# Prologue of a one-core transformer-style block: whole-tile fetches, shared squares and a new order for the first two tiles of x

## The chip, the cores and the metric

The kernel runs on one core of one Trainium2 chip. The metric is the time of one execution on the device in microseconds (us); of several runs the median counts. A profiled execution gives one trace, and all times inside the kernel are counted from the first instruction of that trace.

## What is computed

One layer of a hybrid encoder for 512 frames of width 1024, in float32. Only the very beginning matters here: the first norm and the first block of columns of the combined input projection.

```python
def rms_norm(x, gain):
    xf = x.astype(jnp.float32)
    y = xf * lax.rsqrt(jnp.mean(xf * xf, axis=-1, keepdims=True) + RMS_EPS)
    return (y * gain.astype(jnp.float32)).astype(x.dtype)

h = rms_norm(x, mix_norm_pre[layer])
proj = jnp.einsum("bsd,de->bse", h, w_in[layer])
xa, ga, q, k, v, f_logit, g_a, g_b = jnp.split(proj, offs, axis=-1)
xc = causal_dwconv(xa, conv_a_w[layer], conv_a_b[layer])
...
```

## The kernel before

Five engines work side by side: PE multiplies matrices, ACT (ScalarE), DVE (VectorE) and POOL (GpSimd) do the elementwise work, SP issues most DMAs. Each runs its own list of instructions in order. Float32 products are made from three products of a shorter format: an operand is split into a high part (a rounded copy, made by ACT) and a low part (operand minus high part, made by DVE or POOL), and a product is high x high + high x low + low x high.

The 512 frames lie in four tiles of 128 frames (`xts[0]` to `xts[3]`, 128 x 1024 each). For every tile the prologue makes the sum of squares (`sumsq`, `sumsq_whole`: ACT squares with a running sum, then a square root on ACT and a reciprocal on DVE, `rstd_of`, L233 and L235), scales the tile by that and by the gain (`scaled`, L441, DVE, one half of 512 columns at a time), turns the half by four PE transposes into a PSUM bank (`turn`, L242), copies the high part from there (`evac_hi`, L246, ACT, into `hh`) and makes the low part (`evac_lo`, L250, DVE, into `hl`). The names `us[0]` to `us[3]` are the first four blocks of 128 columns of `w_in`; `us[t].hi()` casts (L172, ACT) and `us[t].lo(pool)` subtracts (L175, POOL). `half(i, lo, hi)` is the product of block i with frames lo to hi: 24 matmuls of 256 columns, the ones with the weight's high part at L457 and L458, those with its low part at L460. The first call, `half(0, 0, 256)`, needs tiles 0 and 1 alone.

The gain is a vector along the 1024 columns, and DVE needs it on every partition. `gone` holds the gain in its columns 0 to 1023 and ones in its last 128 columns, on one row; PE multiplies the ones with the gain (L420), so that two PSUM banks (`pgain`) hold it on all 128 partitions. The gain is fetched by a DMA on ACT's queue (L397), which is followed there by the load of the square root's table and a trial square root (`warm`, L398). `spin` (L415) runs matmuls on an identity matrix whose results nobody reads.

In this prologue the order is written out by hand (`manual_schedule`): each engine gets its instructions in the order of the calls, across all engines' lists. The order before, for tiles 0 and 1 (t, g are tile and half): sumsq(0), scaled(0,0), sumsq(1), us[0].hi and lo, scaled(1,0), turn(0,0), spin(3), turn(1,0), scaled(0,1), turn(0,1), high and low part of (0,0), scaled(1,1), turn(1,1), high and low part of (1,0), (0,1) and (1,1), half(0, 0, 256). Tiles 2 and 3 and the other blocks follow. Tiles 0 and 1 are fetched as two halves each, so SP issues four transfers of 256 KB (L402) and after them the first two weights of 512 KB, tiles 2 and 3, two more weights and the table of constants. PSUM has eight banks; four are asked for first, as sums of the four blocks (`pss`), then two for `pgain`, then one for each turned half.

Of the kernel before, what the change touches and what calls it, by code (L numbers as in the profile page):

```python
# [8 lines left out]
F32 = mybir.dt.float32  # L9
F32R = mybir.dt.float32r  # L10
BF16 = mybir.dt.bfloat16
AF = mybir.ActivationFunctionType
ALU = mybir.AluOpType
# [3 lines left out]
P = 128  # L17
S = 512
D = 1024
KD = D // P  # L20
# [43 lines left out]
def kernel(  # L64
# [15 lines left out]
    nc = tc.nc  # L80
    act, dve, pool, pe = nc.scalar, nc.vector, nc.gpsimd, nc.tensor
# [17 lines left out]
    def bank(name):  # L99
        return pspools[-1].tile([P, 512], F32, tag="ps", name=name)  # L100

    xv = x.rearrange("(t p) d -> p t d", p=P)
    ov = out.rearrange("(t p) d -> p t d", p=P)

    HALVES = (slice(0, 512), slice(512, 1024))
# [180 lines left out]
    hh = hpool.tile([P, KD, S], F32R, name="hh")  # L286
    hl = hpool.tile([P, KD, S], F32R, name="hl")
# [30 lines left out]
    with ExitStack() as rg:  # L318
        rt, ixt, tt = {}, {}, {}
        last_act = [None]  # L320
        with ExitStack() as r0:
# [67 lines left out]
            NF = 4  # L389
            with tc.tile_pool(name="pre", bufs=2, side="right", reuse_waits="tile") as pre:  # L390
# [1 line left out]
                man = ExitStack()  # L392
                man.enter_context(tc.manual_schedule())
                warm = small.tile([P, 1], F32, name="warm", bufs=1)
                gone = pre.tile([1, D + P], F32, name="gone", bufs=1)
                pool.memset(gone[:, D:], 1.0)
                act.dma_start(gone[:, :D], gains[0:1, :])  # L397
                act.activation(out=warm, in_=epst, func=AF.Sqrt)  # L398
                xts = [pre.tile([P, D], F32, tag="xt", name=f"xt{t}", bufs=NT) for t in range(NT)]
                for t in range(2):  # L400
                    for c in HALVES:
                        nc.sync.dma_start(xts[t][:, c], xv[:, t, c])  # L402
                us = [Split(*order[t][1:], order[t][0]) for t in range(2)]
                for t in range(2, NT):
                    nc.sync.dma_start(xts[t], xv[:, t])
                us += [Split(*order[t][1:], order[t][0]) for t in range(2, NF)]
                nc.sync.dma_start(cpt, cp)
                emitted[0] = NF
                pss = [bank(f"xa{t}") for t in range(NF)]

                pw = pss[3]

                def spin(n):
                    for i in range(n):
                        pe.matmul(pw[:, P * (i % 4) : P * (i % 4) + P], ident, ident, start=True, stop=True)  # L415
# [8 lines left out]
                def sumsq(t):  # L424
                    xns[t] = pre.tile([P, D], F32, tag="xn", name=f"xn{t}")
                    s2 = small.tile([P, 2], F32, tag="s2", name=f"s2_p{t}")
                    for i, c in enumerate(HALVES):
                        act.activation(out=xns[t][:, c], in_=xts[t][:, c], func=AF.Square, accum_out=s2[:, i : i + 1])
                    ss = small.tile([P, 1], F32, tag="ss", name=f"ss_p{t}")
                    dve.tensor_tensor(out=ss, in0=s2[:, 0:1], in1=s2[:, 1:2], op=ALU.add)  # L430
                    rss[t] = rstd_of(ss, f"p{t}")

                def sumsq_whole(t):
                    xns[t] = pre.tile([P, D], F32, tag="xn", name=f"xn{t}")
                    ss = small.tile([P, 1], F32, tag="ss", name=f"ss_p{t}")
                    act.activation(out=xns[t], in_=xts[t], func=AF.Square, accum_out=ss)
                    rss[t] = rstd_of(ss, f"p{t}")

                def scaled(t, g):
                    c = HALVES[g]  # L440
                    dve.scalar_tensor_tensor(out=xns[t][:, c], in0=xts[t][:, c], scalar=rss[t], in1=pgain[g],  # L441
                                             op0=ALU.mult, op1=ALU.mult)

                def turn(t, g):
                    ptr[t, g] = turn_block(xns[t], t, g, "p")

                def evac_hi(t, g):
                    lasts[0] = turned_hi(ptr[t, g], t, g, hh)

                def evac_lo(t, g):  # L450
                    lasts[1] = turned_lo(ptr[t, g], t, g, hh, hl)

                def half(i, lo, hi):
                    wh, wl = us[i].parts()
                    ps = pss[i][:, lo:hi]
                    for k in range(KD):
                        pe.matmul(ps, wh[:, k], hh[:, k, lo:hi], start=k == 0, stop=False)  # L457
                        pe.matmul(ps, wh[:, k], hl[:, k, lo:hi], start=False, stop=False)  # L458
                    for k in range(KD):
                        pe.matmul(ps, wl[:, k], hh[:, k, lo:hi], start=False, stop=k == KD - 1)  # L460

                sumsq(0)
                scaled(0, 0)
                sumsq(1)
                us[0].hi()
                us[0].lo(pool)
                scaled(1, 0)
                turn(0, 0)
                spin(3)
                turn(1, 0)  # L470
                scaled(0, 1)
                turn(0, 1)
                evac_hi(0, 0)
                evac_lo(0, 0)
                scaled(1, 1)
                turn(1, 1)
                evac_hi(1, 0)
                evac_lo(1, 0)
                evac_hi(0, 1)
                evac_lo(0, 1)  # L480
                evac_hi(1, 1)
                evac_lo(1, 1)
                half(0, 0, 256)
                us[1].hi()
                us[1].lo(pool)
                sumsq_whole(2)
                scaled(2, 0)
                scaled(2, 1)
# [41 lines left out]
            for t in range(NF, TR + NF):  # L530
# [3 lines left out]
                if t < TR:  # L534
                    ps = bank(f"xa{t}")
# [966 lines left out]
```

## Time and profile before

| | us |
|---|---|
| median of three runs | 928.02 (927.01 to 928.88) |
| profiled execution | 926.11 |
| its span, first to last instruction | 924.2 |
| PE busy | 911.7 (99% of the span) |
| DVE, ACT, POOL busy | 685.2, 568.8, 230.6 |

The page of the profile gives busy times, shares and chains of one execution. An engine's row names the source line, the operation, the tile written and the tiles read, and in brackets the idle time before it with what ended that. PEld is the loading of PE's stationary operand, which runs beside its matmuls; names that end in q (SPq, ACTq) are queues that issue DMAs. Several instructions of one line that follow each other are merged in a timeline; the number behind the x counts them.

### The profile page before, as it was taken

To read this page: it belongs to the slowest core of one execution; us is meant where nothing else is said; L and a number is where in the kernel's file an instruction comes from. 1 tells how busy PE (TensorE), PEld (TensorE's weight loads), DVE (VectorE), ACT (ScalarE), POOL (GpSimd) and SP (SyncE) were. 2 spreads that over 40 slices of the span, in tenths; PEclk is the share of its full clock that TensorE was granted. 3 is DMA by queue.
4 is the path that set the end of the run, shared out by engine and by line. 5 is a ranking of instruction groups with operands and counts; after the bars stand their busy time and mean duration, and the time that the engine had idled before them with its cause. 6 is when DMAs were issued, how large, how long until landed. Compare 5 with 4: busy or idle time off the path is not lost.

```text
span 924.2 us, 14992 instructions
## 1 busy us (share of the span) xinstructions
PE 911.7 (99%) x5582; PEld 796.1 (86%) x5582; DVE 685.2 (74%) x1121; ACT 568.8 (62%) x982; POOL 230.6 (25%) x240
## 2 busy tenths in 40 slices
PE   8999999999999999999999999999999999999996
PEld 7988888887888888888888889999999999978885
DVE  5866369632857777777644588999999999889897
ACT  7555495433345566666423376688888888676664
POOL 4134345444242232220111000042323323100001
PEclk9999999999999999999999999999999999999998
DMA  7677589989776566553232755188898888799764
GB/s 278 216 227 208 165 207 256 270 211 253 176 229 152 160 148 157 151 150 86 69 114 91 271 182 163 34 212 235 218 238 204 234 208 211 223 372 325 240 201 142
DMA packets 76282, 182.29 MB, mean 197 GB/s; under 512 B 7281, under 2 KB 35745, under 8 KB 75826
## 3 DMA queue, kind: packets, MB, share of 16 engines
q1 hardware_dynamic: 45056, 123.13, 39.5%
q0 software_dynamic: 30864, 57.68, 30.2%
q8 instruction: 44, 0.72, 0.3%
q10 hardware_dynamic: 290, 0.53, 0.1%
q14 instruction: 28, 0.23, 0.1%
HBM read 148.59 MB, written 33.64 MB: 197 GB/s over the span
## 4 chain that ended last, share of the span: by engine, by line
PE 94%; DVE 2%; DMA 1%; issue 1%; ACT 0%; POOL 0%; SPq 0%; DVEq 0%; POOLq 0%
PE up L924 7%; PE up L922 7%; PE up L921 7%; PE dn L1225 4%; PE dn L1224 4%; PE dn L1223 4%; PE pa L223 2%; PE ga L224 2%; PE ga L223 2%; PE pa L224 2%; PE pa L222 2%; PE ga L222 2%; PE q L222 2%; PE ma L222 2%; PE wo L838 2%; PE mb L222 2%
## 5 line engine op out<-in xcount | busy, mean ns | idle before, releaser
L868 POOL DMA_DIRECT2D ml<-raw_up x41 | 35.0, 855 | 154.8 <-ACT ml L867 79.2
L1076 DVE SCALAR_TENSOR_TENSOR u<-up,cpt,u 128x511 f32<-128x511 f32 x96 | 71.2, 745 | 2.6 <-ACT u L1070 0.9
L1225 PE MATMUL dn<-wh_dn,al 128*128 128x512 f32 x168 | 65.6, 391 | 0.9 <-DVE al L845 0.8
L1224 PE MATMUL dn<-wl_dn,ah 128*128 128x512 f32 x168 | 65.4, 389 | 0.0
L1223 PE MATMUL dn<-wh_dn,ah 128*128 128x512 f32 x168 | 65.4, 389 | 0.0
L921 PE MATMUL up<-sh,th 128*128 128x256 f32 x252 | 60.4, 277 | 0.5 <-ACT x L928 0.5
L922 PE MATMUL up<-sl,th 128*128 128x256 f32 x252 | 60.2, 276 | 0.0
L175 DVE TENSOR_TENSOR wl_dn<-raw_dn,wh_dn 128x1024 fp32r<-128x1024 f32 x42 | 51.5, 1226 | 9.1 <-ACT wh_dn L172 9.1
L172 ACT CAST wh_dn<-raw_dn 128x1024 fp32r<-128x1024 f32 x42 | 44.1, 1050 | 17.5 <-issue 10.3
L845 DVE TENSOR_TENSOR tl<-t,th 128x1024 fp32r<-128x1024 f32 x42 | 51.1, 1218 | 1.3 <-ACT th L902 1.3
L1084 POOL TENSOR_TENSOR yf<-u,u 128x512 f32<-128x512 f32 x24 | 32.0, 1333 | 71.8 <-issue 47.5
L1070 ACT ACTIVATE u<-up,cpt 128x512 f32<-128x512 f32 x48 | 36.9, 778 | 19.8 <-PE up L924 11.0
L921 PEld LDWEIGHTS up<-sh,th 128*128 128x128 f32 x252 | 47.3, 188 | 0.7 <-ACT x L928 0.7
L922 PEld LDWEIGHTS up<-sl,th 128*128 128x128 f32 x252 | 47.3, 188 | 0.0
L902 ACT CAST th<-t 128x1024 fp32r<-128x1024 f32 x42 | 43.9, 1045 | 4.5 <-DVE t L845 1.8
L689 POOL DMA_DIRECT2D B<-maskf x32 | 39.1, 1628 | 27.2 <-DMA B<-cnd 24.1
L922 PE MATMUL up<-h2l,mh 128*128 128x256 f32 x168 | 40.2, 276 | 0.0
L921 PE MATMUL up<-h2h,mh 128*128 128x256 f32 x168 | 40.2, 276 | 0.0
L924 PE MATMUL up<-sh,tl 128*128 128x256 f32 x252 | 38.8, 276 | 0.0
L1225 PEld LDWEIGHTS dn<-wh_dn,al 128*128 128x128 f32 x168 | 31.5, 188 | 8.1 <-DVE al L845 1.7
L175 DVE TENSOR_TENSOR wl_pa<-raw_pa,wh_pa 128x640 fp32r<-128x640 f32 x16 | 13.1, 819 | 32.8 <-ACT wh_pa L172 32.8
L1224 PEld LDWEIGHTS dn<-wl_dn,ah 128*128 128x128 f32 x168 | 31.5, 188 | 6.6
(654 smaller groups left out, 3167.7 us busy)
## 6 DMA issues: line engine op xcount, KB each, us to landing
raw_up<-in_w_up_dram SPq DMA_DIRECT2D x48, 512.0 KB, 5.4
td<-in_w_down_dram POOLq DMA_DIRECT2D x36, 512.0 KB, 5.9
raw_dn<-td SPq DMA_DIRECT2D x24, 512.0 KB, 5.0
B<-cnd POOLq DMA_DIRECT2D x16, 640.0 KB, 4.8
ml<-raw_up POOLq DMA_DIRECT2D x20, 512.0 KB, 5.3
raw_dn<-in_w_down_dram SPq DMA_DIRECT2D x18, 512.0 KB, 3.5
raw_wo<-in_w_out_dram SPq DMA_DIRECT2D x16, 512.0 KB, 3.8
td<-td POOLq DMA_DIRECT2D x12, 512.0 KB, 10.8
```

Source lines behind the costliest of these rows:

```text
L172: act.copy(self.wh, self.raw)
L175: engine.tensor_tensor(out=self.wl, in0=self.raw, in1=self.wh.bitcast(F32), op=ALU.subtract)
L222: pe.matmul(dst, ah, bh, start=first, stop=False)
L845: dve.tensor_tensor(out=out, in0=a, in1=b, op=ALU.subtract)
L902: act.copy(self.th[i], self.t[i])
L921: pe.matmul(dst, wh[:, k], ah[:, k], start=first and k == 0, stop=False, skip_group_check=True)
L922: pe.matmul(dst, wh[:, k], al[:, k], start=False, stop=False, skip_group_check=True)
L924: pe.matmul(dst, wl[:, k], ah[:, k], start=False, stop=k == KH - 1, skip_group_check=True)
L1076: dve.scalar_tensor_tensor(out=c[:, s:], in0=ps[:, : S - s], scalar=col(C_CFW + 3 * e + j), in1=c[:, s:], op0=ALU.mult, op1=ALU.add)
L1223: pe.matmul(dst[t], ah[:, k, tok], wh[:, k], start=first, stop=False, skip_group_check=True)
L1224: pe.matmul(dst[t], ah[:, k, tok], wl[:, k], start=False, stop=False, skip_group_check=True)
L1225: pe.matmul(dst[t], al[:, k, tok], wh[:, k], start=False, stop=last, skip_group_check=True)
```

## The change

Tiles 0 and 1 are fetched by one transfer of 512 KB each. `gone` gets 128 rows: DVE clears columns 0 to 1023 of all of them, the gain is fetched into row 0 behind that, and the ones fill 128 rows, so the vector's matmuls contract over 128 rows of which 127 are zero. Tile 0's squares are made half by ACT and half by DVE (a multiply with a running sum); tile 1's squares are made by ACT in one instruction. Both halves of tile 0 are scaled before anything of tile 1, then turned and copied in that order; `us[0].hi()` and `lo` come next, then tile 1's halves; the four low parts of tiles 0 and 1 come last. The three fillers (six instructions) between transposes go; the four at the start stay. Of the four sums' PSUM banks two are asked for at the beginning and two behind the first product. `half` issues all matmuls with `hh`, then all with `hl`, where it alternated before; their number is the same.

```diff
--- before.py
+++ after.py
@@ -392,23 +392,23 @@
                 man = ExitStack()
                 man.enter_context(tc.manual_schedule())
                 warm = small.tile([P, 1], F32, name="warm", bufs=1)
-                gone = pre.tile([1, D + P], F32, name="gone", bufs=1)
+                gone = pre.tile([P, D + P], F32, name="gone", bufs=1)
+                dve.memset(gone[:, :D], 0.0)
                 pool.memset(gone[:, D:], 1.0)
-                act.dma_start(gone[:, :D], gains[0:1, :])
+                act.dma_start(gone[0:1, :D], gains[0:1, :])
                 act.activation(out=warm, in_=epst, func=AF.Sqrt)
                 xts = [pre.tile([P, D], F32, tag="xt", name=f"xt{t}", bufs=NT) for t in range(NT)]
                 for t in range(2):
-                    for c in HALVES:
-                        nc.sync.dma_start(xts[t][:, c], xv[:, t, c])
+                    nc.sync.dma_start(xts[t], xv[:, t])
                 us = [Split(*order[t][1:], order[t][0]) for t in range(2)]
                 for t in range(2, NT):
                     nc.sync.dma_start(xts[t], xv[:, t])
                 us += [Split(*order[t][1:], order[t][0]) for t in range(2, NF)]
                 nc.sync.dma_start(cpt, cp)
                 emitted[0] = NF
-                pss = [bank(f"xa{t}") for t in range(NF)]
-
-                pw = pss[3]
+                pss = [bank(f"xa{t}") for t in range(2)]
+
+                pw = pss[1]
 
                 def spin(n):
                     for i in range(n):
@@ -424,8 +424,10 @@
                 def sumsq(t):
                     xns[t] = pre.tile([P, D], F32, tag="xn", name=f"xn{t}")
                     s2 = small.tile([P, 2], F32, tag="s2", name=f"s2_p{t}")
-                    for i, c in enumerate(HALVES):
-                        act.activation(out=xns[t][:, c], in_=xts[t][:, c], func=AF.Square, accum_out=s2[:, i : i + 1])
+                    a, b = HALVES
+                    act.activation(out=xns[t][:, a], in_=xts[t][:, a], func=AF.Square, accum_out=s2[:, 0:1])
+                    dve.tensor_tensor_reduce(out=xns[t][:, b], in0=xts[t][:, b], in1=xts[t][:, b], scale=1.0, scalar=0.0,
+                                             op0=ALU.mult, op1=ALU.add, accum_out=s2[:, 1:2])
                     ss = small.tile([P, 1], F32, tag="ss", name=f"ss_p{t}")
                     dve.tensor_tensor(out=ss, in0=s2[:, 0:1], in1=s2[:, 1:2], op=ALU.add)
                     rss[t] = rstd_of(ss, f"p{t}")
@@ -453,36 +455,32 @@
                 def half(i, lo, hi):
                     wh, wl = us[i].parts()
                     ps = pss[i][:, lo:hi]
-                    for k in range(KD):
-                        pe.matmul(ps, wh[:, k], hh[:, k, lo:hi], start=k == 0, stop=False)
-                        pe.matmul(ps, wh[:, k], hl[:, k, lo:hi], start=False, stop=False)
+                    for h in (hh, hl):
+                        for k in range(KD):
+                            pe.matmul(ps, wh[:, k], h[:, k, lo:hi], start=h is hh and k == 0, stop=False)
                     for k in range(KD):
                         pe.matmul(ps, wl[:, k], hh[:, k, lo:hi], start=False, stop=k == KD - 1)
 
                 sumsq(0)
                 scaled(0, 0)
-                sumsq(1)
+                scaled(0, 1)
+                sumsq_whole(1)
+                for g in range(2):
+                    turn(0, g)
+                    evac_hi(0, g)
                 us[0].hi()
                 us[0].lo(pool)
-                scaled(1, 0)
-                turn(0, 0)
-                spin(3)
-                turn(1, 0)
-                scaled(0, 1)
-                turn(0, 1)
-                evac_hi(0, 0)
-                evac_lo(0, 0)
-                scaled(1, 1)
-                turn(1, 1)
-                evac_hi(1, 0)
-                evac_lo(1, 0)
-                evac_hi(0, 1)
-                evac_lo(0, 1)
-                evac_hi(1, 1)
-                evac_lo(1, 1)
+                for g in range(2):
+                    scaled(1, g)
+                    turn(1, g)
+                    evac_hi(1, g)
+                for g in range(2):
+                    for t in range(2):
+                        evac_lo(t, g)
                 half(0, 0, 256)
                 us[1].hi()
                 us[1].lo(pool)
+                pss += [bank(f"xa{t}") for t in range(2, NF)]
                 sumsq_whole(2)
                 scaled(2, 0)
                 scaled(2, 1)
```

## Rows read from the trace of the kernel before

**Rows 1.** Busy time of each engine by stretch; then granted clock and DMA share.
```profile
14.00:918.80 904.80, 900.27 (x5539) 788.24 (x5539) 677.55 (x1106) 559.74 (x964) 227.36 (x231) 1.00 0.70 196
```

**Rows 2.** PE's waits over the whole run: total, times, longest.
```profile
PE up L924 <- DMA ml<-raw_up: 0.9, 1, 0.9
PE dn L1225 <- DVE al L845: 0.8, 1, 0.8
```

**Rows 3.** Chain that ended last, 0 to 16 us: start, duration, what.
```profile
2.13 5.59 DMA xt<-in_x_dram
...
14.00 0.38 PE xa L458
```

**Rows 4.** Timeline of all engines, 0 to 24 us; "x" counts merged instructions.
```profile
0.74 0.53 ACTq L397 DMA_DIRECT2D gone<-in_gains_dram  x1
...
0.74 1.81 SPq L402 DMA_DIRECT2D xt<-in_x_dram  x4
...
1.30 1.28 ACT L398 ACT_TABLE_LOAD   x1 [1.30 <-PEq L1489]
...
3.50 3.78 PE L420 MATMUL gain<-gone 1*128 1x512 f32 x4
...
3.92 0.63 ACT L428 ACTIVATE xn<-xt 128x512 f32<-128x512 f32 x1 [1.12 <-DMA xt<-in_x_dram]
...
4.60 0.63 ACT L428 ACTIVATE xn<-xt 128x512 f32<-128x512 f32 x1
...
6.14 0.75 DVE L441 SCALAR_TENSOR_TENSOR xn<-xt,rs_p,gain 128x512 f32<-128x512 f32 x1
...
7.21 1.11 PE L242 MATMUL tr_p<-ident,xn 128*128 128x128 f32 x4
...
8.11 1.49 PE L415 MATMUL xa<-ident 128*128 128x128 f32 x6
...
8.98 1.04 ACT L172 CAST wh_xa<-raw_xa 128x1024 fp32r<-128x1024 f32 x1
...
10.10 2.37 POOL L175 TENSOR_TENSOR wl_xa<-raw_xa,wh_xa 128x1024 fp32r<-128x1024 f32 x1 [8.67 <-ACT wh_xa L172]
...
11.09 1.08 ACT L246 CAST hh<-tr_p 128x512 fp32r<-128x512 f32 x2 [0.59 <-PE tr_p L242]
...
11.80 1.28 DVE L250 TENSOR_TENSOR hl<-tr_p,hh 128x512 fp32r<-128x512 f32 x2
...
14.06 1.06 ACT L436 ACTIVATE xn<-xt 128x1024 f32<-128x1024 f32 x1
...
14.94 1.12 PE L460 MATMUL xa<-hh,wl_xa 128*128 128x256 f32 x8
...
15.77 1.40 DVE L441 SCALAR_TENSOR_TENSOR xn<-xt,rs_p,gain 128x512 f32<-128x512 f32 x2
...
15.90 0.28 PE L457 MATMUL xa<-hh,wh_xa 128*128 128x256 f32 x1
...
18.78 1.91 PE L242 MATMUL tr_p<-ident,xn 128*128 128x128 f32 x16
```

**Rows 5.** DMA queues to 2.0 us; issues at 1.7 and at 2.5 us, with landing.
```profile
q10 hardware_dynamic: 2, 0.00, 0.8%
...
xt<-in_x_dram SPq DMA_DIRECT2D x1, 256.0 KB, 3.6
...
raw_xa<-in_w_in_dram SPq DMA_DIRECT2D x1, 512.0 KB, 6.4
xt<-in_x_dram SPq DMA_DIRECT2D x1, 256.0 KB, 5.6
```

**Rows 6.** Transposes (L242) of 10.88 to 11.6 us: duration min/median/max, starts.
```profile
L242 PE MATMUL tr_p<-ident,xn x6: 273/273/421, 10.5 to 11.2; 128*128 128x128 f32 x6
```

**Rows 7.** Groups on DVE: line, form, count; busy us, mean ns.
```profile
L175 DVE TENSOR_TENSOR wl_xa<-raw_xa,wh_xa 128x1024 fp32r<-128x1024 f32 x1 | 1.2, 1224 | 2.1 <-ACT wh_xa L172 2.1
...
L719 DVE CUSTOM_DVE_ANT_0 P<-s2c,B 128x512 f32<-128x512 f32 x1 | 0.7, 692 | 0.0
```


## The prediction

> **What bounds the kernel now.** The page's busy table names TensorE (PE) as the bound; I went on to the table of stretches to see where its pauses lie. Between 14.0 and 918.8 us PE works 900.27 of 904.80 us [rows 1]. So whatever the first stage gives PE earlier is kept, unless one of the few later waits takes it. The list of PE's waits has the two largest of those: 0.9 us for a DMA at L924 and 0.8 us for DVE at L1225 [rows 2]; both hang on work that PE's own progress paces, so I expect them to move along with PE.
>
> The change is all in the first 16 us, so there I read the chain of work that ended last [rows 3]. It stands 5.59 us on the transfer of x, then goes through ACT (squares), DVE (scaling of tile 1's first half, of tile 0's second, a low part, scaling of tile 1's second half), PE (transposes), ACT (high part) and DVE (low part) to PE's L458 at 14.00. From there it is PE alone. The timeline gives the two marks that I count with: the first product `half(0, 0, 256)` ends with its eight L460 matmuls from 14.94, and `half(1, 0, 256)` starts at 15.90 [rows 4]. Everything in front of 15.90 is the latency of the first two tiles of x, and the change is worth as much as it moves that mark.
>
> The landing times say which tile is late. Tile 0's first half is issued at 0.74 and has landed when its square starts at 3.92 [rows 4]. The third transfer, tile 1's first half, is issued some 0.9 us after the first and takes 3.6 us [rows 5], to about 5.3; the fourth is issued at 2.13 [rows 3] and takes 5.6 us [rows 5], to 7.7.
>
> The granted clock is 1.00 for 14 to 918.8 us [rows 1]; for the start I read it from matmuls of one form. Four transposes take 1.11 us at 7.21 and sixteen 1.91 us at 18.78, 0.28 against 0.12 us each [rows 4], about a factor of two, as between 1.2 and 2.4 GHz. Around 10.9 us their duration falls from 421 to 273 ns [rows 6], so the clock rises there. Before that rise PE ran fillers, the vector's matmuls at 3.50, transposes, six filler instructions at 8.11 and transposes again.
>
> **The change part by part, against the span of the profiled execution.**
>
> *The vector.* DVE now clears 128 x 1024 before the gains are fetched. No such memset is in the trace. DVE's 128x1024 subtraction at 1.22 us [rows 7] is the nearest row and bounds it above, since it reads two tensors and this reads none; zero bounds it below. I take 1.0, from 0.74 to 1.74; DVE has nothing else to do before tile 0's squares are summed. The 0.53 us trigger on ACT's queue waits for it. Behind it on ACT stand the table load (1.28), `warm` and the first square; the load now starts at 1.30, right behind the trigger [rows 4], and is moved by 1.0 with it; `warm` (under 0.3) ends at 3.8 or 3.9, just before the square's start at 3.92, so this costs nothing. With the memset at 1.22 it would cost 0.2. The transfer itself was done within 1.3 us of its issue (its two packets are counted in the stretch up to 2.0 us [rows 5]), so it lands at 3.0 if nothing stands before it, and at 1.74 + 3.2 = 4.9 if it is served like a half of x (3.92 - 0.74). PE is at the fillers until 3.50 anyway. I take a start of the vector's matmuls at 3.8, nearer to its own row than to x's, with 3.5 and 4.9 as ends. They take 3.78 us in all [rows 4] with 128 rows as with one, since they stream the same 512 columns: first bank ready about 5.9, both at 7.6.
>
> The Trainium skill ("DMA: Bandwidth & Descriptors", section on queues, rings and completion order) says that a DMA engine takes turns between queues, but drains a whole packet of one before it turns to the next. No row shows two queues in competition here. By it the vector would wait behind x, which is the rival "late vector" below.
>
> *Transfers of x.* Two triggers less on SP, some 0.45 us each (four lie between 0.74 and 2.6), so every transfer behind tile 0 is issued 0.45 (x tile 1) to 0.9 us earlier (the weights, tiles 2 and 3). The bytes stay. Tile 0 whole lands between 3.9 (its half) and 4.6 (where the second square could start without waiting); I take 4.4. Tile 1 lands between 5.3 and 7.7; I take 6.5, the middle. The first weight landed at 2.6 + 6.4 = 9.0 [rows 5] and comes at 8.5 to 9.0.
>
> *Tile 0's squares.* ACT's second half (0.63) goes to DVE, whose reduce of 128x512 takes 0.69 (L719, [rows 7]); both run side by side. From the second square's start to the first scaling there are 6.14 - 4.60 = 1.54 us now; so scaling starts at 4.4 + 1.55 = 5.95, when the vector's first bank is just there. The second scaling needs the vector's second bank: 7.6 to 8.35.
>
> *Tile 1.* One square of 128x1024; from such a square's start to its scaling the trace has 15.77 - 14.06 = 1.71 us [rows 4]. 6.5 + 1.7 = 8.2, and DVE is free at 8.35: scalings 8.4 to 9.8. A landing at 7.7 would make it 9.4, which the next step hides but for 0.1 to 0.3 us.
>
> *ACT's order.* After tile 0's second half is scaled, PE turns it at the low clock (1.11, to 9.5), ACT makes the high part (0.59, to 10.1), and then `us[0].hi()` stands in the way: 1.04 us, to 11.1, after which alone tile 1's high parts run (two in 1.08 [rows 4], to 12.1). This is a cost of the new order: the cast used to lie at 8.98, in front of the first high part. Its weight is landed by then, so no DMA wait comes with it; POOL's low part of that weight (behind the cast, 2.4 us [rows 4]) ends at 13.5, just in time for L460.
>
> *DVE's low parts.* Tile 0's first is made at 9.8; the other three follow tile 1's high part at 11.6, 0.6 us apart (two in 1.28 [rows 4]), the last done at 13.45.
>
> *The product.* `half` now issues eight matmuls with hh, eight with hl, eight with the weight's low part, 24 as before. The hh ones run from 11.6 as the high parts arrive, the first four hl ones too; the last four wait for 13.5, take 0.47, then eight L460: 13.5 + 0.47 + 0.96 = 14.9. `half(1, 0, 256)` then starts at 14.9 instead of 15.90: **-1.0 us**. The wait inside the first product, at L458 before 14.00 [rows 3], gives way to the one for 13.5.
>
> *No price.* The later request for two PSUM banks: two sums, two vector halves and four transposed blocks are eight, and the next is wanted at about 17.8, long after the low parts. Fillers gone: PE would be waiting for DVE there anyhow, so they hide nothing but the clock (rival below).
>
> **Sum.** 926.11 (profiled execution, span 924.2 and 1.9 around it) - 1.0 = 925.1. The median lies 1.91 above the profiled execution, so 928.02 - 1.0 = **927.0**.
>
> **Rivals.**
>
> *The clock rises earlier* because the vector's matmuls now use 128 rows: for it, the full-array fillers and transposes went before the only rise seen, and the one-row vector did not bring it; against, one rise proves no cause. Then turning tile 0's second half takes 0.66 instead of 1.11 and the vector's second bank comes up to 0.4 earlier: another -0.8, **926.2**.
>
> *Late vector.* It lands at 4.9; both scalings of tile 0 and all behind them move by 1.1: 16.0 instead of 14.9, **928.1**. For it: its transfer was issued with x's first one before and now starts when x's packets flow. Against: it is one packet.
>
> *The clock stays at 1.2 GHz through the first products*, the case that ends slower. The six filler instructions at 8.11 stood shortly before the rise at 10.9, and they go; what PE does from 8 to 11 us is transposes. A matmul of 256 columns then takes some 0.22 instead of 0.12. Started at 11.6, `half(0)` breaks even if the clock rises at about 14.7; if it rises at 18, `half(0)` ends at 16.9 and `half(1)` at 20.3 instead of 18.8: +1.5, **929.5**; with both products wholly slow it is 3.4 more than now. Against: the transposes are as many as before and closer together, and the vector's matmuls are now full ones.
>
> The Trainium skill ("TensorE: Matmul & The Clock Gate", Part 4) says that the full clock does not engage for transposes; by it this rival's result would be the likelier one. The trace bears neither out: fillers and transposes both precede its rise.
>
> *Later waits swallow it.* The two waits of [rows 2] are 0.8 and 0.9 us; if one of them grows by what PE gains, the time stays at **928.0**. Against: the transfers there are issued as buffers come free, thus by PE's progress.
>
> **How the numbers follow.** Forecast (927.0) 0.45, earlier clock (926.2) 0.20, late vector (928.1) 0.15, clock stays low (929.5) 0.12, swallowed (928.0) 0.08. A measurement of this kernel can tell some 0.2% from no change, 1.86 us: 926.2 and 929.9 are the limits. The earlier clock lies on the limit, half of it beyond; a twentieth of each other case may fall there through the later waits: faster 0.15. The slow clock reaches 929.9 in over half of its span (1.5 to 3.4): slower 0.08. Same 0.77. The range: down to 927.0 - 0.8 - 0.5 (a later wait smaller by half) = 925.7; up to 928.9, which takes in the late vector with 0.8 for a later wait and leaves out most of the slow clock.
>
> **What would show it.** Right: `half(1, 0, 256)` starts near 14.9, four low parts on DVE run in a row from about 10 to 13.5, and the chain leads from the vector's matmuls through `us[0].hi()`. Wrong: the vector's matmuls start after 4.5 (late vector); transposes of 421 ns or 256-column matmuls of over 0.2 us apart after 11 us (clock); ACT's first square held up by the table load (memset longer than taken); the mark moved but the end not (later waits).

## The result and the profile after

The changed kernel takes 931.8 us (median of 13 runs, 928.81 to 933.55) against 928.21 us of the kernel before (13 runs, 927.01 to 930.5): 1.0035 times as long, 95% interval 1.0023 to 1.0046. It is slower, by 2 to 4 us, where 927.0 was forecast. The profiled execution of the changed kernel took 929.2 us with a span of 927.4, that of the kernel before 926.11 with 924.2: 3.2 us more from first to last instruction.

The same table of stretches as [rows 1], of the changed kernel (busy us and instructions of PE, PEld, DVE, ACT, POOL, then granted clock, DMA share, GB/s):

```profile
15.40:923.20 907.80, 900.55 (x5538) 788.17 (x5536) 679.64 (x1109) 559.66 (x964) 227.93 (x232) 1.00 0.69 195
```

PE works as long as before behind the start (900.55 against 900.27 us). The ends of such a stretch are chosen, not measured; PE's last matmul starts at 916.12 before and at 919.24 after, 3.1 us later. PE's waits, to be held against [rows 2] (total us, times, longest):

```profile
PE gain L420 <- DMA gone<-in_gains_dram: 2.9, 1, 2.9
PE gate L376 <- DMA halo_h<-xl: 1.6, 1, 1.6
...
PE dn L1223 <- DVE al L843: 0.8, 1, 0.8
...
PE up L922 <- DMA ml<-raw_up: 0.5, 1, 0.5
```

Two waits are new: for the gains at L420, and for `halo_h` at L376. The two that the prediction watched are there and no longer than before. The start of the changed kernel in the timeline, to be held against [rows 4]:

```profile
1.02 0.91 DVE L396 MEMSET gone<- 128x1024 f32 x1 [1.02 <-PEq L1487]
...
1.97 0.52 ACTq L398 DMA_DIRECT2D gone<-in_gains_dram  x1
...
4.34 0.63 ACT L428 ACTIVATE xn<-xt 128x512 f32<-128x512 f32 x1 [0.32 <-DMA xt<-in_x_dram]
4.34 0.69 DVE L429 CUSTOM_DVE_ANT_0 xn<-xt 128x512 f32<-128x512 f32 x1 [2.40 <-DMA xt<-in_x_dram]
...
5.59 1.06 ACT L438 ACTIVATE xn<-xt 128x1024 f32<-128x1024 f32 x1
...
6.49 3.75 PE L420 MATMUL gain<-gone 128*128 128x512 f32 x4 [2.91 <-DMA gone<-in_gains_dram]
...
8.57 0.75 DVE L443 SCALAR_TENSOR_TENSOR xn<-xt,rs_p,gain 128x512 f32<-128x512 f32 x1 [2.74 <-PE gain L420]
10.03 0.69 PE L242 MATMUL tr_p<-ident,xn 128*128 128x128 f32 x4
10.28 0.75 DVE L443 SCALAR_TENSOR_TENSOR xn<-xt,rs_p,gain 128x512 f32<-128x512 f32 x1 [0.96 <-PE gain L420]
...
12.26 1.05 ACT L172 CAST wh_xa<-raw_xa 128x1024 fp32r<-128x1024 f32 x1
...
13.83 1.89 DVE L250 TENSOR_TENSOR hl<-tr_p,hh 128x512 fp32r<-128x512 f32 x3 [0.68 <-ACT hh L246]
...
17.30 0.88 PE L460 MATMUL xa<-hh,wh_xa 128*128 128x256 f32 x6
```

Tile 0's squares start at 4.34 on both engines and its factor is ready at 5.83, but PE stands 2.91 us for the gains, and DVE then stands 2.74 and 0.96 us for the vector's two banks. The mark, `half(1, 0, 256)`, starts at 17.30 instead of 15.90 [rows 4]: +1.40 us. The chain that ended last (start, us, what), against [rows 3], runs through the new things:

```profile
1.02 0.92 DVE gone L396
...
1.97 4.38 DMA gone<-in_gains_dram
...
6.49 3.77 PE gain L420 x4
...
10.28 0.76 DVE xn L443
...
12.36 0.95 ACT wh_xa L172
...
13.83 1.90 DVE hl L250 x3
...
36.78 1.14 DVE wl_xa L175
37.92 3.29 DVE xc L333 x5
...
42.04 5.02 DMA halo_h<-xl
...
47.10 0.50 PE gate L376
```

So the loss in the two profiled executions is 1.40 (the mark) and 1.59 (the wait at L376, exact duration), 2.99 of 3.2 us. No engine's own list of instructions changes behind the prologue; what follows is the same work 3 us later.

**What happens at L376.** Behind the prologue the columns of xa continue block by block. In each block POOL copies one column of that block's high part into a small tile (`background`, L149, tile `tick`) and then issues a transfer of 512 KB between DRAM tensors (L127, `td`). SP copies rows of finished tiles into `halo_h` (L365), 32 to 128 KB each, and PE reads that at L376. The DMA issues of the third `td` and of these copies (KB, us from issue to landing), first of the kernel before (38.5 to 41 us), then of the changed one (40 to 42.2 us):

```profile
td<-in_w_down_dram POOLq DMA_DIRECT2D x1, 512.0 KB, 4.6
halo_h<-xh SPq DMA_DIRECT2D x2, 64.0 KB, 3.6
halo_h<-xl SPq DMA_DIRECT2D x1, 64.0 KB, 3.1
```

```profile
td<-in_w_down_dram POOLq DMA_DIRECT2D x1, 512.0 KB, 6.2
halo_h<-xh SPq DMA_DIRECT2D x2, 64.0 KB, 5.6
halo_h<-xl SPq DMA_DIRECT2D x1, 64.0 KB, 5.0
```

Before, that `td` is issued at 38.70 and lands at 43.3; the copies land at 43.7 and 43.9, and PE, which waits for nothing, comes to L376 at 44.04: 0.13 us of slack, which no list of waits shows. In the changed kernel the `td` lands at 46.3, the copies at 46.5 to 47.06, and PE has stood since 45.51. In both traces the copies land just behind the `td`. It lands later because the one ahead of it was issued later. Rows of POOL and DVE around that issue, first before, then after:

```profile
35.40 0.18 POOL L149 COPY tick<-wh_xa 128x1 f32<-128x1 f32 x1 [2.12 <-ACT wh_xa L172]
35.60 1.22 DVE L175 TENSOR_TENSOR wl_xa<-raw_xa,wh_xa 128x1024 fp32r<-128x1024 f32 x1 [0.23 <-issue]
35.85 0.51 POOL L127 DMA_DIRECT2D td<-in_w_down_dram  x1 [0.28 <-issue]
```

```profile
36.70 1.22 DVE L175 TENSOR_TENSOR wl_xa<-raw_xa,wh_xa 128x1024 fp32r<-128x1024 f32 x1
36.80 1.16 POOL L149 COPY tick<-wh_xa 128x1 f32<-128x1 f32 x1 [2.11 <-ACT wh_xa L172]
37.90 0.51 POOL L127 DMA_DIRECT2D td<-in_w_down_dram  x1
```

POOL's copy and DVE's subtraction are released by the same cast on ACT. Before, DVE pauses 0.23 us ("issue": it waits for nothing that the profile shows), POOL goes first and its copy takes 0.18 us. After, DVE starts at once, and the copy, 0.10 us behind it, takes 1.16 us and ends with the subtraction; the `td` behind it is issued 2.05 us later than before, 0.65 more than the mark's 1.40. The Trainium skill ("SBUF — State Buffer", Who interferes with whom) says that a DVE instruction with two inputs in SBUF contends with a POOL instruction that reads SBUF, and that the order of issue decides who blocks; these rows agree, with 0.18 and 1.16 us.

### The profile page after: what moved, and what is told of

Read it like the earlier page. It is cut to its first block, busy times and chain, and to the rows that moved or that the text cites. A ratio compares the mean times of both kernels' runs of the same rounds, so it can differ in the third digit from the quotient of the medians.

```text
span 927.4 us, 14977 instructions
## 1 busy us (share of the span) xinstructions
PE 910.3 (98%) x5576; PEld 794.5 (86%) x5576; DVE 687.6 (74%) x1123; ACT 567.8 (61%) x978; POOL 230.8 (25%) x240
## 4 chain that ended last, share of the span: by engine, by line
PE 92%; DVE 3%; DMA 2%; issue 1%; ACT 1%; POOL 0%; DVEq 0%; SPq 0%; POOLq 0%; ACTq 0%
PE up L922 7%; PE up L919 6%; PE up L920 6%; PE dn L1223 4%; PE dn L1221 4%; PE dn L1222 4%; PE pa L223 2%; PE ga L224 2%; PE ga L223 2%; PE pa L224 2%; PE pa L222 2%; PE ga L222 2%; PE q L222 2%; PE ma L222 2%; PE wo L836 2%; PE mb L222 2%
## 5 line engine op out<-in xcount | busy, mean ns | idle before, releaser
L175 DVE TENSOR_TENSOR wl_dn<-raw_dn,wh_dn 128x1024 fp32r<-128x1024 f32 x42 | 51.5, 1227 | 8.7 <-ACT wh_dn L172 8.6
L900 ACT CAST th<-t 128x1024 fp32r<-128x1024 f32 x42 | 43.9, 1046 | 5.2 <-DVE t L843 2.3
L175 DVE TENSOR_TENSOR wl_pa<-raw_pa,wh_pa 128x640 fp32r<-128x640 f32 x16 | 13.1, 819 | 32.8 <-ACT wh_pa L172 32.8
```

What stands on the lines that cost most here:

```text
L175: engine.tensor_tensor(out=self.wl, in0=self.raw, in1=self.wh.bitcast(F32), op=ALU.subtract)
L900: act.copy(self.th[i], self.t[i])
```

## The experiments

Three theories were tested. **Late vector**: the gains are fetched behind a memset, meet x's transfers and make the mark late. **Halo**: the wait at L376 is a second loss, made by who goes first at L149 and L175 and independent of the mark. Rival to both: the new order itself (squares, scalings, low parts) costs the time. A fourth question was the clock, whose granted value was 0.995 or 0.996 in six of the changed kernel's 13 runs and never below 0.997 in the 90 runs of the kernel before that were taken with the experiments. This mean also holds the end of an execution, where the granted clock is 0.50 behind PE's last matmul (918.80 to 924.20 us in the kernel before); so 0.995 and 0.996 point to a fall on the way, and 0.997 alone settles nothing: the trace of experiment 11 has 0.997 with a fall, that of the kernel before without. The mark below is the start of `half(1, 0, 256)`; "before" is the median of the runs of the kernel before that belong to the same experiments.

**1. The change without its vector.** One row, no memset.

```diff
-                gone = pre.tile([P, D + P], F32, name="gone", bufs=1)
-                dve.memset(gone[:, :D], 0.0)
+                gone = pre.tile([1, D + P], F32, name="gone", bufs=1)
...
-                act.dma_start(gone[0:1, :D], gains[0:1, :])
+                act.dma_start(gone[:, :D], gains[0:1, :])
```

> The changed kernel with the vector's part undone: one row, no clearing by DVE, the rest of the change kept. Late-vector theory (the clearing by DVE, and then a transfer served behind x, hold the vector's matmuls from 3.5 to 6.49 us, and this moves half(1, 0, 256) from 15.90 to 17.30): the vector's matmuls start at 3.5 again, half(1, 0, 256) at 14.6 to 15.0, and the time falls to about 1.0 us under that of the kernel before (927.2 beside 928.2). If instead the order, the whole-tile fetches or the missing fillers cost the time: the mark stays at 17 or later and the time stays 3 us above.

928.0 us against 927.08, ratio 1.0008 (0.9998 to 1.0018). The mark is at 14.80, 1.10 us earlier than before; the prediction's 14.9 for the change. But L376 waits:

```profile
PE gate L376 <- DMA halo_h<-xl: 1.3, 1, 1.3
```

So the new order is no loss: it brings the 1.1 us, and the wait at L376 takes it back. The clock takes more in some executions: five of the 12 have a granted clock of 0.996 and a median of 929.13 us, the seven others one of 926.65, 0.4 under the kernel before. That wait is there although the mark is early, so it doesn't come from a late mark.

**2. The vector alone**, put into the kernel before.

```diff
-                gone = pre.tile([1, D + P], F32, name="gone", bufs=1)
+                gone = pre.tile([P, D + P], F32, name="gone", bufs=1)
+                dve.memset(gone[:, :D], 0.0)
...
-                act.dma_start(gone[:, :D], gains[0:1, :])
+                act.dma_start(gone[0:1, :D], gains[0:1, :])
```

> The kernel before with the vector's part of the change alone (128 rows, cleared by DVE first). Late-vector theory: the gain lands at 5 to 6.5 us, PE waits for it some 2 to 3 us, the scaling of tile 0's second half cannot start before 9 to 10.3, and half(1, 0, 256) starts 0.5 to 1.2 us later than 15.90; the time is 0.5 to 3 us above the kernel before, the upper end if the wait for the halo at 47 us comes with it. If the order or the fetches cost the time: no change, 928.2.

928.94 us against 927.08, 1.0019 (1.0008 to 1.003). The vector's matmuls start at 5.18:

```profile
5.18 1.19 PE L421 MATMUL gain<-gone 128*128 128x512 f32 x1 [1.60 <-DMA gone<-in_gains_dram]
```

The mark is at 15.74, no later than before: in the old order, tile 0's second half was scaled behind tile 1's first, at 9.88 only, so a late vector hides there. The loss is a wait of 1.2 us at L376, and in four of the 11 executions a granted clock of 0.995 or 0.996 with it (median 930.4, the seven others 928.0). Late vector and new order don't add up: -0.16 and -1.10 each alone, +1.40 together.

**3. The vector in time.** The changed kernel, with the gains fetched at once into a row of their own, from where DVE copies them into the cleared block.

```diff
+                grow = pre.tile([1, D], F32, name="grow", bufs=1)
+                act.dma_start(grow, gains[0:1, :])
                 dve.memset(gone[:, :D], 0.0)
...
-                act.dma_start(gone[0:1, :D], gains[0:1, :])
+                dve.tensor_copy(out=gone[0:1, :D], in_=grow)
```

> The changed kernel, 128 rows kept, but the gain is fetched at once into a row of its own and copied into the cleared block by DVE, so that no transfer waits for the clearing. Late-vector theory: as with one row, the vector's matmuls start at 3.5 to 4.2 us, the mark lies at 14.6 to 15.5 and the time is 0 to 1.3 us under that of the kernel before. If 128 rows matter for the clock: transposes of 273 ns before 10 us and a mark up to 0.8 us earlier than with one row; if not: transposes of 421 ns until about 10 us in both.

926.6 us against 927.08, 0.9995 (0.9987 to 1.0004). The copy starts at 2.20, so the row had landed 1.5 us after its issue at 0.74; issued at 1.97 in the changed kernel, it took 4.38. The vector's matmuls start at 3.37 and the mark is at 14.04, 1.86 us earlier than before and 3.26 earlier than after. Little of that reaches the end: L376 waits 2.2 us, and behind the wait the granted clock falls (columns as above):

```profile
40.00:44.84 4.84, 2.69 (x12) 1.91 (x12) 4.62 (x6) 3.44 (x4) 1.60 (x2) 1.00 0.49 157
44.84:48.26 3.42, 3.42 (x10) 2.65 (x9) 2.08 (x4) 2.42 (x5) 0.88 (x1) 0.50 0.91 325
48.26:52.00 3.74, 3.74 (x18) 3.09 (x17) 1.79 (x3) 0.06 (x1) 0.40 (x1) 1.00 0.22 57
```

For 3.42 us PE runs at the lower level, 1.2 GHz: 10 matmuls where the next 3.74 us hold 18. Two of the 11 executions had a granted clock of 0.996 or less; their median is 928.68, that of the others 926.49.

**4. Late mark alone.** The kernel before with nine more fillers ahead of `half(0, 0, 256)`.

```diff
+                spin(9)
                 half(0, 0, 256)
```

> The kernel before with nine more fillers (18 instructions, some 2 us) in front of half(0, 0, 256), so that half(1, 0, 256) starts at about 17.3 as in the changed kernel, with everything else as before. Theory of a second cost (the shift lets the halo transfers of 41 us meet other transfers, and PE then waits 1.6 us at L376): time 3 us above the kernel before and a wait at L376 in the trace. If a shift costs only itself: 1.4 us above, no such wait.

929.02 us against 927.08, 1.0022 (1.0013 to 1.0032), with the mark at 17.92, 2.0 us later than before. A late mark goes to the end about one to one. DVE's pause and the short copy are there as in the kernel before, and the wait at L376 is 0.6 us. That wait has another beginning: the copy of `xl` is issued at 44.11, where a shift of 2.0 us from 40.82 would put it at 42.8, because the issue ahead of it on SP took 1.87 us instead of 0.58; why is open. The profiled execution, 929.02, is the median by chance; that of the kernel before lies 1.0 under the median, so mark and wait together (2.6) are to be held against 2.9 there.

**5. to 7. Without the transfers that `halo_h` meets.** The three `td` of the first xa blocks are put off by some blocks, in the changed kernel (5), in experiment 3 (6) and, as a control, in the kernel before (7).

```diff
-                if t > NF:
+                if t > NF + 3:
                     background(1, u)
...
-            background(2, w)
+            background(5 if t == 0 else 2, w)
```

> The changed kernel with three of POOL's background transfers of 512 KB (issued at 34 to 40 us there) put off to the first block of the ga stage; the vector is still late. Theory of the second cost (the halo transfers are served behind these, PE waits 1.6 us for them at L376, and in some executions the clock then falls for 3.4 us): no wait at L376 in the trace, no execution with a mean clock under 0.997, and the time falls from 3 to 4 us above the kernel before to about 1.4 above, the late vector's part alone. If the wait at L376 has another cause: it stays, and so does the time.

> The changed kernel with the gain fetched at once into a row of its own (as e3) and the three background transfers put off. With both costs gone the earlier mark of 14.0 us should reach the end: 1.9 us under the kernel before (0.2%), no wait at L376, no execution with a mean clock under 0.997. If something else at 44 us bounds the stage: no better than e3, 0.5 us under.

> The kernel before with the three background transfers put off alone, the control for the two above. PE waits for no halo in its profile, so: no change within 0.5 us. If executions of the kernel before that are not profiled do wait there: up to 0.7 us faster.

| | us | against before (927.13) | mark | wait at L376 |
|---|---|---|---|---|
| 5: changed kernel, `td` put off | 927.84 | 1.0003 (0.9995 to 1.0012) | 17.05 | none |
| 6: vector in time, `td` put off | 924.63 | 0.9974 (0.9965 to 0.9984) | 13.68 | none |
| 7: kernel before, `td` put off | 926.32 | 0.9991 (0.9982 to 0.9999) | 15.96 | none |

The wait at L376 is gone in all three, and no run of theirs has a granted clock under 0.997. With it, the difference between changed kernel and kernel before shrinks from 3.6 us to 927.84 - 926.32 = 1.5 us, about the 1.1 us between their marks. With the vector in time as well, 6 lies 1.7 us under 7 (marks: 2.3), and 2.5 us under the kernel before: a version faster than both. The control was forecast within 0.5 us of the kernel before and is 0.8 under it; some of that kernel's executions may wait at L376 though its profile does not, but no trace shows it. The copies' landing in 5 shows what they had met:

```profile
halo_h<-xh SPq DMA_DIRECT2D x2, 64.0 KB, 2.0
halo_h<-xh SPq DMA_DIRECT2D x1, 128.0 KB, 2.2
```

2.0 us instead of the 5.6 of the changed kernel.

**8. A late `td` in the kernel before.** Its second tick reads the low part, so that it comes behind DVE's subtraction; nothing of the prologue is touched.

```diff
-                    background(1, u)
+                    background(1, u[::-1] if t == NF + 2 else u)
```

> The kernel before in which POOL's second copy of this stage (the one in front of a background transfer at 35.4 us) reads the low part of the weight instead of the high part, so that it comes behind DVE's subtraction as in the traces of the changed kernel and of e1 to e3 (there the copy lasts 1.16 us instead of 0.18, since DVE's subtraction has started 0.1 us ahead of it). Theory of the tie between POOL and DVE: the transfer is issued 1.2 us later, meets the halo transfers, and PE waits about 1.2 us at L376: 1.2 us slower, more where the clock falls. If the tie doesn't matter: no change.

931.68 us (six runs) against 927.13, 1.0042 (1.0028 to 1.0056), with the mark at 16.00. The wait at L376 is 2.5 us and the clock falls behind it:

```profile
42.00:46.80 4.80, 2.27 (x11) 1.59 (x9) 4.80 (x7) 3.61 (x5) 1.60 (x2) 1.00 0.68 206
46.80:50.21 3.41, 3.41 (x8) 2.66 (x9) 1.66 (x3) 1.79 (x4) 0.25 (x1) 0.50 0.83 321
```

Five of the six runs had a granted clock of 0.995 or 0.996 (median 931.8), the sixth took 927.85. So the time of one `td` is worth 4.5 us, more than the whole change cost. It is issued at 37.51, 1.66 us later than in the kernel before, against the 0.65 beyond the mark in the changed kernel; the run shows the mechanism and not its size there.

**9. One more instruction on DVE.** The kernel before, with a memset of the tick tile (59 ns at 0.81 us, for which nothing waits there).

```diff
                 pool.memset(gone[:, D:], 1.0)
+                dve.memset(tick, 0.0)
```

> The kernel before, with one more instruction on DVE ahead of everything: a memset of the small tile that POOL's ticks write to; nothing waits for it in the prologue, and it is done long before the first tick, so half(1, 0, 256) should start at 15.9 plus or minus 0.3 as before. Theory A (which of two engines released together goes first hangs on how many instructions DVE has behind it: with one more, DVE's subtraction at L175 starts ahead of POOL's tick): the tick near 35 us takes about 1.2 us instead of 0.18, PE waits 0.8 to 1.6 us for halo_h at L376, and the time is 0.8 to 3 us above the kernel before. Theory B (what goes first hangs on when PE came there, that is on the later mark): the tick takes 0.18 us, there is no wait of over 0.3 us at L376, and the time is within 0.5 us of the kernel before.

929.23 us against 927.68, 1.002 (1.0009 to 1.0031). DVE's pause is gone and with it POOL's lead:

```profile
34.73 1.23 DVE L175 TENSOR_TENSOR wl_xa<-raw_xa,wh_xa 128x1024 fp32r<-128x1024 f32 x1
...
34.84 1.17 POOL L149 COPY tick<-wh_xa 128x1 f32<-128x1 f32 x1 [2.12 <-ACT wh_xa L172]
```

PE waits 1.8 us at L376, as theory A had it; the mark is at 15.33, 0.27 us ahead of the range expected, so the loss is not the prologue's. So an instruction that has been done for 34 us costs 1.5 us, through the order of the pair.

**10. One instruction less on DVE**, in experiment 1: as many as in the kernel before.

```diff
-                    dve.tensor_tensor(out=ss, in0=s2[:, 0:1], in1=s2[:, 1:2], op=ALU.add)
+                    act.activation(out=ss, in_=s2[:, 0:1], func=AF.Identity, bias=s2[:, 1:2])
```

> As e1_one_row (the changed kernel with the vector from one row), but the two sums of squares of tile 0 are added on ACT instead of DVE, so that DVE has one instruction less ahead of the second background, as many as in the kernel before. half(1, 0, 256) should start near 14.8 plus or minus 0.3. Theory A (the count of DVE's instructions decides who goes first): POOL's tick takes 0.18 us, the wait at L376, 1.3 us in e1_one_row, is 0.3 us or less, and the time is 0.7 to 1.3 us below the kernel before. Theory B (the earlier mark itself makes the halo late): the wait at L376 stays at 0.9 to 1.5 us and the time within 0.4 us of the kernel before.

928.52 us against 927.68, 1.0005 (0.9995 to 1.0015); the copy takes 1.17 us and PE waits 2.0 us at L376. Theory A falls in its form: the count of instructions is not what decides. Theory B's numbers don't come either (a wait of 0.9 to 1.5 us, a time within 0.4). What the traces do show is where DVE's pause stands. In the kernel before and experiments 4, 7 and 8, whose DVE lists are the same, it is there, 0.21 to 0.23 us; in the eight others up to here (after, 1 to 3, 5, 6, 9, 10) DVE starts without one. It isn't POOL that holds DVE up: in 7 no tick comes at all.

```profile
35.66 1.22 DVE L175 TENSOR_TENSOR wl_xa<-raw_xa,wh_xa 128x1024 fp32r<-128x1024 f32 x1 [0.21 <-issue]
```

So the kernel before owed its missing wait to a pause of 0.2 us in its own list of DVE instructions. What makes the pause stays open.

**11. Whole tiles or halves.** Experiment 6 with tiles 0 and 1 fetched as halves again.

```diff
-                    nc.sync.dma_start(xts[t], xv[:, t])
+                    for c in HALVES:
+                        nc.sync.dma_start(xts[t][:, c], xv[:, t, c])
```

> As f2_early_row_postponed, but tiles 0 and 1 of x are fetched as halves again. If the whole-tile fetch is what brings tile 1 earlier, its landing goes from about 5.7 back to 6.8 to 7.7 us, half(1, 0, 256) starts 0.1 to 0.5 us later than there (13.7) and the time is 0 to 0.5 us longer. If something else brought it (the triggers saved for the vector), nothing of this moves by over 0.1 us.

925.64 us against 927.68, 0.9983 (0.9974 to 0.9993): 2.0 us under the kernel before on the same chip, where experiment 6 was 2.5 under it on another. The two intervals overlap, so medians tell little here; the profiled executions differ by 1.6 us (925.64 and 924.04). Tile 1's square starts, as its data land, at 7.42 instead of 5.55, so the whole-tile fetch brings 1.9 us. More than expected comes out of it: the mark is at 15.45, 1.77 later. PE stands 1.7 us for tile 1's scaling, and the clock, up since 6.53, is at 0.50 again from 9.95 to 13.36:

```profile
6.53:9.95 3.42, 1.61 (x9) 0.84 (x8) 2.07 (x5) 2.50 (x6) 0.00 (x0) 1.00 0.99 376
9.95:13.36 3.41, 3.34 (x15) 3.15 (x16) 2.78 (x5) 2.79 (x4) 2.38 (x1) 0.50 1.03 422
```

**12. The fillers.** Experiment 6 with the three fillers between the transposes back.

```diff
+                spin(3)
```

> As f2_early_row_postponed, but with the fillers between the transposes back. If the fillers no longer have a use (the clock rises behind the vector's 128-row matmuls), the clock rises at 6 to 7 us in both, the start of half(1, 0, 256) stays within 0.3 us of 13.7 and the time within 0.5 us. If the fillers did serve the clock, the mark comes 0.3 to 1 us earlier; if they only stand in the way, 0.3 to 1 us later.

924.01 us against 927.68 (four runs), 0.9961 (0.9948 to 0.9974); mark 13.76 against 13.68. The interval overlaps that of experiment 6, and the times lie within its scatter (923.73 to 926.0): nothing lost with the fillers, nothing gained that these runs can tell.

## Why the prediction was wrong

**The vector's landing**, the step that failed first. The memset was sized well (taken 1.0 us; 0.91, with the trigger at 1.97 where 1.74 was taken), and the table load moved by 1.2 us without holding up the first square, as said. The landing was bounded by 3.0 and 4.9; it came at 6.35 (1.97 and 4.38 in the chain). The upper end was made from a half of x (3.2 us), a row of before, when the gains went out together with x's first half. Now they go out behind the memset, and the change itself puts more ahead of them: two tiles and the first weight, of 512 KB each, are issued by then. In experiment 2, where three halves of 256 KB are, PE could start at 5.18, 1.3 us sooner. The DMA queues of the changed kernel show the wait (packets, MB, share of the engines' time): first from 2 to 5.6 us, then, the second row, from 5.6 to 5.8 us. q10 is the gains' queue as in [rows 5], q1 that of x and the weights.

```profile
q1 hardware_dynamic: 336, 1.25, 97.2%
```

```profile
q10 hardware_dynamic: 1, 0.00, 5.0%
```

In the kernel before both packets of the gains were done by 2.0 us [rows 5]; here none has run by 5.6 us, when tile 1 has just landed (5.57). The estimate's own working gives what followed: late by 6.49 - 4.9 = 1.6 us against its "late vector" (mark 16.0), it would be 17.6; the trace has 17.30. The rival was right in kind, with 0.15, and its price bounded too low. The Trainium skill's rule on queues ("DMA: Bandwidth & Descriptors", queues, rings and completion order), put there as speaking for this rival, agrees in so far as the gains did wait behind x. That the wait would last 3.6 us and 336 packets does not follow from it, and no row here tells the 16 DMA engines apart, so what set its length is open.

**Everything else up to the mark** held. With the vector taken out the mark was at 14.80 (forecast 14.9). Tile 0 landed at 4.31 (taken 4.4), tile 1 at 5.57 (taken 6.5, a miss of 0.9 in the change's favour that the vector's second bank hid), weight 0 before its cast. `us[0].hi()` stood where it was said to stand, and the last three low parts ran in a row at 13.83 and led to the end of the first product, as the chain has it. The chain of experiment 1, with the vector out of the way, ends the cast of `us[0].hi()` at 10.8 (forecast 11.1) and the low parts at 13.2 (13.5). PSUM banks and fillers cost nothing that was seen.

**The clock.** The rival "stays at 1.2 GHz" is out: the transposes of the changed kernel's first half take 0.69 us for four at 10.03, against 1.11 before [rows 4], and the first products run at 1.00. The rival "rises earlier" was right: with 128 rows and the vector in time the rise comes at 7.30, 6.11, 6.53 and 4.50 (experiments 3, 6, 11 and 12), with one row at 10.26 to 13.43 (before, 1, 4, 7 to 10), with 128 rows and the vector late at 10.20, 9.56 and 9.85 (after, 2, 5). A rise here is the start of the trace's first record of the granted clock; the tables of stretches show 1.00 ahead of it too, where the durations of [rows 6] show the lower level. In experiments 3, 6, 11 and 12 the vector's matmuls start at 3.37 alike and PE does the same work until its first transposes, yet the rises lie 2.8 us apart: that it comes earlier is shown, by how much only roughly. The rival's -0.8 is what experiment 3's mark has over experiment 1's: 14.04 against 14.80. In the changed kernel itself the late vector hid it (rise at 10.20). Of the Trainium skill's sentence that the full clock does not engage for transposes ("TensorE: Matmul & The Clock Gate", Part 4), experiment 10 shows the contrary for the float32 transposes of this kernel (the page's durations are for bf16, and no row says whether these run in the mode that it means): between 7.2 and 10.7 us PE ran transposes alone, and their mean went from 409 ns (8.9 to 10.2 us) to 321 ns (10.2 to 11.3 us) as the clock rose at 10.26:

```profile
L242 PE MATMUL tr_p<-ident,xn 128*128 128x128 f32 x8 | 1.9, 409 | 0.0
...
L242 PE MATMUL tr_p<-ident,xn 128*128 128x128 f32 x4 | 0.8, 321 | 0.0
```

**Later waits**, the step that failed second, and the larger one. The first paragraph took it that what PE gains or loses at the start is kept, unless one of the waits of [rows 2] takes it. Those two did nothing. A place that was in no list, because PE came 0.13 us behind the landing, took 1.6 us. The list of waits says where PE stood, not where it nearly stood. And the sentence that later transfers are issued by PE's progress, so that all moves along, was wrong at that place: one of them is issued behind a POOL copy whose length, 0.18 or 1.16 us, hangs on 0.1 us. That the order of that pair brings the wait is shown in the kernel before (experiments 8 and 9); a version of the changed kernel in which POOL goes first was tried in 10 and did not come about, so there it is argued from the rows and from experiment 5, where the wait goes with the transfers.

**The sum, closed.** Profiled executions: +1.40 (mark) and +1.59 (L376), 2.99 of 3.2 us. Medians: +3.6, of which 1.5 remain without the wait (experiments 5 and 7). The other 2.1 are the wait and, in the six executions with a granted clock of 0.995 or 0.996, what follows it: these have a median of 932.8, the seven others 930.7, so the fall costs about 2 us where it comes. That it is the wait at L376 that brings it is shown in two traces (experiments 3 and 8) and by its absence from all runs of 5, 6 and 7; the profiled execution of the changed kernel has the wait without the fall.

## What to carry over

Before a change to the start of a kernel is priced, look not only at the waits but at the landings just ahead of the instructions that did not wait: a slack of 0.1 us at a DMA became a wait of 1 to 2 us here as soon as two engines swapped places. A small transfer that everything hangs on is issued before the large ones, into a buffer that nothing has to clear first; here a memset ahead of its trigger cost 1.2 us of issue time and 2.9 us more in flight. And a change that loses can hold a good part: undone piece by piece, this one gave a kernel 2.5 us faster than the one before.

## What was not expected of the hardware

- A copy of one column on POOL takes 0.18 us or 1.16 us, by whether it starts ahead of or 0.10 us behind a DVE subtraction of 128 x 1024 (1.22 us).
- One DVE instruction of 59 ns, done 34 us earlier, decided which of the two starts first; the pause of 0.2 us that it removed has no cause in the profile.
- A row of 4 KB lands 1.5 us after its issue at 0.74 us and 4.4 us after one at 1.97 us, behind two transfers of 512 KB on another queue (landed at 4.31 and 5.57).
- The granted clock fell to 0.50 for 3.4 us behind waits of PE of 2.2, 2.5 and 1.7 us (experiments 3, 8 and 11), and did not in the profiled executions with waits of 1.2 to 2.0 us at L376 (after, 1, 2, 9, 10).
